# Moving the tiles of a two-block attention kernel so that TensorE's operands start on 256-byte boundaries of SBUF

## The chip, the cores and the metric

One core of a Trainium2 chip runs the program. The metric is the device time of one execution in microseconds. The kernel before took 1605.19 us (median of 3 runs, 1604.76 to 1605.27).

## The reference

Two transformer blocks follow each other on a 512 x 2048 float32 input. The first is sliding-window attention with sinks: a norm, one projection to queries, keys, values and a gate, 32 heads of 64 with a window of 128, a gated output and an output projection, added to the input. The second puts 16 learned tokens ahead of the 512 and runs differential attention (8 heads) and latent attention with rotary positions (8 heads) side by side, again gated, projected and added, with a last norm.

```
h = rms_norm(x, swa_norm);  q, k, v, gate = split(h @ w_in)
o = softmax_with_sink(q k^T / 8 + bias, window 128) v
x = x + (o * silu(gate)) @ w_out
h = concat(meta, x);  proj = rms_norm(h) @ w_in_2          # 528 rows, 5952 columns
oA = rms_norm((softmax(q1 k1) - lam * softmax(q2 k2)) vA) ;  oB = softmax(qB kB + rope) vB
h = h + concat(oA * silu(gA), oB * silu(gB)) @ w_out_2
y = rms_norm(h, final_norm)
```

## The kernel before, in words

Every large product is made of three matmuls. An operand is kept as two float32r tiles, a rounded high part and the low rest (names ending in h and l, or `xh1`/`xl1`, `xh2`/`xl2`), and a product is high x high + high x low + low x high, through the helper `mm` (L111). Weights come in by DMA on SP's queue as 512 KB pieces `raw`; ScalarE copies a 128 x 512 unit to `wh` (L158) and VectorE makes `wl` (L168). In each matmul one operand stands in the array (a 128 x 128 block, which TensorE loads with a LDWEIGHTS instruction) and the other moves through it (up to 512 columns).

The stages run one after another on TensorE; attention pieces are woven into the projections by a queue of deferred functions (`Flow`), and VectorE, ScalarE and TensorE work in the order of the program text.

1. Keys, values and queries of block one (to about 300 us): the weights move, the input `xh1`/`xl1` stands (`proj_n`, L288 on). 960 matmuls with 512 columns, and woven in the window attention: scores with 256 columns (`kth`, `ktl` move, `qt` stands), transposes, and 112 products p x v with 512 columns.
2. Gate of block one, `gate1` (about 300 to 509 us): the input moves, the weights stand (`proj_t`). 768 matmuls with 512 columns.
3. Output of block one, `out1` (509 to 694 us): weights move, `ogh1`/`ogl1` stand. 768 with 512 columns. Its result is transposed into `xh2`/`xl2`, the input of block two.
4. Latent projections (`c_cq`, `c_ck`, `c_pe`): weights move and `xh2`/`xl2` stand (192 with 512 columns, 240 with 320), then 48 with 512 columns.
5. Heads of block two (about 800 to 1270 us): `diff_qk` (384 with 512 columns and 768 with 264), `diff_v` (768 with 264), `mla_proj` (96 with 512 columns, others with 256 and 264), with the attention of 16 heads woven in.
6. Gates of block two, `gate2` (about 1270 to 1420 us): `xh2`/`xl2` move, weights stand. 768 with 512 columns. Rows k = 0 to 15 of the input are taken in turn, 12 matmuls for one k (k = 0, 1 and 14, 15 in another order).
7. Output of block two, `out2` (from 1420 us): weights move, `ogh2`/`ogl2` stand. 720 with 512 columns and 96 with 256. Its first 7 units of weights still come from the tiles that all earlier stages use; then `open_ring` gives it a ring of 16 new `wh` and 16 new `wl`.

Of the 8615 matmuls that the page counts, 4864 have 512 columns; the others are shorter or are transposes.

The positions of tiles in SBUF come out of the code in this way. A pool with side "left" grows up from the low end of SBUF, one with side "right" down from the high end; tiles of a pool lie one behind the other in the order in which the code first asks for them, each rounded up to 32 bytes. So sizes in the code give the positions. The remainder of the byte address by 256 in the program before, called the phase here:

| tile | phase |
|---|---|
| `raw`, `wh`, `wl` (all stages) | 160 |
| `wh`, `wl` of the ring in `out2` | 192 |
| `xh1`, `xl1` | 160 |
| `ogh1`, `ogl1` | 224 |
| `ogh2`, `ogl2` | 192 |
| `xh2`, `xl2` | 160; one row k takes 528 floats = 2112 bytes = 8 x 256 + 64, so the 512 token columns of row k start at phase 224 + 64k: 224, 32, 96, 160, 224, ... |
| `kth`, `ktl`, the values `v` | 64 |
| `qt` | 192 |
| `pth`, `ptl` of block one | 224 |
| `cqh`, `cql`, `ckh` | 160 |
| `identr` | 128 |

A block of 128 columns of a standing operand is 512 bytes and a weight unit 2048 bytes, so all blocks of a tile have its phase (rows of `xh2` apart). The halves of 264 columns in `diff_qk` and `diff_v` start at the row and 1056 bytes behind it.

Of the kernel before, what the change touches and what calls it, by code (L numbers as in the profile page):

```python
# [9 lines left out]
F32 = mybir.dt.float32  # L10
F32R = mybir.dt.float32r
# [7 lines left out]
KT = 16  # L19
S = 512  # L20
NTB = 4
META = 16
LK = S + META
HALF = LK // 2
EPS = 1e-6
BIG = 1e30
ZROW = 384
# [8 lines left out]
def mixer_kernel(ctx, tc, x, rel_bias, w_in1, q_gain, k_gain, sinks, w_out1,  # L36
# [37 lines left out]
    P = Pools()  # L74
    dram = P("dram", space=DRAM)
    const = P("const", side="left")
    wp = P("w", side="left")
    ps_pj = P("ps_pj", bufs=4, space=PSUM)
    ps_sc = P("ps_sc", bufs=2, space=PSUM)
    ps_tp = P("ps_tp", bufs=2, space=PSUM)  # L80
# [183 lines left out]
    F = Flow()  # L264
# [97 lines left out]
    rstd2 = const.tile([128, NTB], F32, name="rstd2")  # L362
    mrstd = const.tile([128, 1], F32, name="mrstd")
    nlam = const.tile([128, 1], F32, name="nlam")
    G1, G2, GQ, GKV, GSUB = 0, 16, 32, 36, 38

    xa = P("xa", side="left")
# [150 lines left out]
    p1 = P("p1", side="right")  # L518
# [2 lines left out]
    vt = [p1.tile([128, 4, 2, 64], F32R, name=f"v{t}") for t in range(NTB)]  # L521

    def hstat():
        return p1.tile([128, 8], F32, tag="st", name="st", bufs=4)

    def qn_t():
        return p1.tile([128, 512], F32, tag="qn", name="qn", bufs=4)
# [110 lines left out]
    def swa_pieces():  # L638
        items = [(g, t, i) for g in range(4) for t in range(NTB) for i in range(2)]
        st = {}  # L640

        def s1(n, j):
            g, t, i = items[n]
            if t == 1 and i == 0 and j == 0 and g < 3:
                swa_bias(g + 1)
            if j == 0:
                st[n] = dict(
                    p=p1.tile([128, 4, 256], F32, tag="p", name="p", bufs=2),
                    nm=p1.tile([128, 4], F32, tag="nm", name="nm", bufs=3),
                    sm=p1.tile([128, 4], F32, tag="sm", name="sm", bufs=3))  # L650
            p, nm, sm = st[n]["p"], st[n]["nm"], st[n]["sm"]
            qt = qts[g, t]
            bias = biases[g, i]
            h0 = 8 * g + 4 * i
            k0 = max(t - 1, 0) * 128
            lo = 128 if t == 0 else 0
            w = 256 - lo
            sc = ps_sc.tile([128, 2, 256], F32, tag="sc", name="sc")
            for a in range(2):
                h = 4 * i + 2 * j + a  # L660
                mm(sc[:, a, :], qt[:, h, :], kth[:, g, k0:k0 + 256], True, False)
                mm(sc[:, a, :], qt[:, h, :], ktl[:, g, k0:k0 + 256], False, True)
            for a in range(2):
                b = 2 * j + a
                nc.vector.tensor_tensor_reduce(  # L665
                    out=p[:, b, :w], in0=sc[:, a, :w], in1=back(bias, b, w), scale=1.0,
                    scalar=nsink[:, h0 + b:h0 + b + 1], op0=ALU.add, op1=ALU.min,
                    accum_out=nm[:, b:b + 1])
                nc.scalar.activation(out=p[:, b, :w], in_=p[:, b, :w], func=ACTF.Exp, scale=-1.0,  # L669
                                     bias=nm[:, b:b + 1], accum_out=sm[:, b:b + 1])  # L670
            if j == 1:
                es = p1.tile([128, 4], F32, tag="es", name="es", bufs=3)
                st[n]["es"] = es
                nc.vector.tensor_tensor(out=es, in0=nm, in1=nsink[:, h0:h0 + 4], op=ALU.subtract)
                nc.scalar.activation(out=es, in_=es, func=ACTF.Exp)
# [125 lines left out]


    xb = P("xb", side="left")
    xh2 = xb.tile([128, KT, LK], F32R, tag="h", name="xh2")
    xl2 = xb.tile([128, KT, LK], F32R, tag="l", name="xl2")
    XR = {}

    def open_xr():
# [12 lines left out]
    def meta_in():  # L821
        xr_p = XR["p"]
        mt = xr_p.tile([16, D], F32, name="mt")
        nc.sync.dma_start(out=mt, in_=meta)
        mps = xr_p.tile([128, KT, 16], F32, name="mps")
        nc.sync.dma_start(out=mps, in_=meta_t)
        mss = xr_p.tile([16, 1], F32, name="mss")
        mjunk = xr_p.tile([16, D], F32, name="mjunk")

        def rest():  # L830
            nc.scalar.activation(out=mjunk, in_=mt, func=ACTF.Square, accum_out=mss)
            rsqrt_mean(mrstd[:16], mss, D, rows=16)
            mg = xr_p.tile([128, KT, 16], F32, name="mg")
            nc.vector.tensor_tensor(
                out=mg, in0=mps, in1=gcols[:, G2:G2 + 16].unsqueeze(2).to_broadcast([128, KT, 16]),
                op=ALU.mult)
            split(xh2[:, :, 0:16], xl2[:, :, 0:16], mg)
            row_bcast(rb2[:, 0:16], mrstd, 16)
        F.defer(20, rest)

    def out1(c):
        if c:
            XR[c] = load_r(c)
        ps = [pj() for _ in range(NTB)]

        def evac(t):
            xr_p, ss2, xr = XR["p"], XR["ss"], XR[c]
            nc.vector.tensor_tensor(out=xr[:, t, :], in0=ps[t], in1=xr[:, t, :], op=ALU.add)
            squares(xr, c, ss2, xr_p, t)
            if t == NTB - 1:  # L850
                for i in range(4):
                    F.defer(4 + 2 * i, lambda i=i: x_to_t(xr, c, i, xh2, xl2, META, G2))
                if c == 3:
                    F.defer(13, finish)
                F.defer(14, lambda: nc.sync.dma_start(
                    out=x1_d[:, c * 512:(c + 1) * 512].rearrange("(t p) c -> p t c", p=128), in_=xr))

        def finish():
            ssr2 = XR["p"].tile([128, NTB], F32, name="ssr2")
            nc.vector.tensor_reduce(out=ssr2, in_=XR["ss"], axis=AX.X, op=ALU.add)  # L860
            rsqrt_mean(rstd2, ssr2, D)
            F.defer(6, lambda: [row_bcast(rb2[:, 16 + t * 128:16 + (t + 1) * 128], rstd2[:, t:t + 1])
                                for t in range(NTB)])

        proj_n(c_o1[c], KT, lambda k, b: (og["h"][:, k, b * 128:(b + 1) * 128],
                                          og["l"][:, k, b * 128:(b + 1) * 128]), ps, evac)
# [9 lines left out]


    def tok(k, b):
        c = slice(META + b * 128, META + (b + 1) * 128)
        return xh2[:, k, c], xl2[:, k, c]  # L880

    def tok_m(k, b):
        if b < NTB:
            return tok(k, b)
        return xh2[:, k, 0:128], xl2[:, k, 0:128]

    B2 = {}

    def open_b2():
        P.close("xr", "og1")  # L890
        ms = P("ms", side="left")
        B2["cqh"] = ms.tile([128, 4, S], F32R, name="cqh")
        B2["cql"] = ms.tile([128, 4, S], F32R, name="cql")
        CW = 2 * LK + 256
        B2["ckh"] = ms.tile([128, CW], F32R, name="ckh")
        B2["ckl"] = ms.tile([128, CW], F32R, name="ckl")
        for n_ in ("ckh", "ckl"):
            nc.gpsimd.memset(f32(B2[n_][:, 2 * LK:]), 0.0)
        B2["kph"] = ms.tile([128, LK], F32R, name="kph")
        B2["kpl"] = ms.tile([128, LK], F32R, name="kpl")  # L900
        B2["qpt"] = ms.tile([128, 8, S], F32R, name="qpt")
        p2c = P("p2c", side="right")
        lat = P("lat", side="right")
        for nm_, shape, src in (
                ("relm", [128, LK], c_rel), ("mask", [128, LK], c_mask),
                ("cosq", [128, NTB, 32], c_cos[META:, :].rearrange("(t p) c -> p t c", p=128)),
                ("sinq", [128, NTB, 32], c_sin[META:, :].rearrange("(t p) c -> p t c", p=128)),
                ("cosm", [16, 32], c_cos[:META, :]), ("sinm", [16, 32], c_sin[:META, :])):
            t = (p2c if shape[1] == LK else lat).tile(shape, F32, name=nm_)
            nc.sync.dma_start(out=t, in_=src)  # L910
            B2[nm_] = t
        B2["rsub"] = p2c.tile([128, 32], F32, name="rsub")
        B2["p2c"] = p2c
        B2["lat"] = lat
# [160 lines left out]
        return [lambda k: src(k, slice(0, HALF)), lambda k: src(k, slice(HALF, LK))]  # L1075

    def xk(k, c):
        return xh2[:, k, c], xl2[:, k, c]

    def ckx(k, c):  # L1080
# [5 lines left out]
    def mla_proj(h):  # L1086
        p2 = B2["p2"]
# [3 lines left out]
        ql = p2.tile([128, S], F32R, tag="mql", name="mql", bufs=1)  # L1091
        kh = p2.tile([128, LK], F32R, tag="mkh", name="mkh", bufs=1)
        kl = p2.tile([128, LK], F32R, tag="mkl", name="mkl", bufs=1)
        cq_, ckv = c_m[h]
        pq = pj()
        proj_t(cq_, 4, [(slice(0, 128), [(pq, lambda k: (B2["cqh"][:, k, :], B2["cql"][:, k, :]))],
# [40 lines left out]
    def diff_qk(h):  # L1137
# [5 lines left out]
        def qev():  # L1143
# [3 lines left out]
            qd = [p2.tile([128, S], F32R, tag=f"dq{i}", name=f"dq{i}", bufs=1) for i in range(2)]  # L1147
            ql = B2["qlz"]
            ks = [p2.tile([128, LK], F32R, tag=f"dk{i}", name=f"dk{i}", bufs=1) for i in range(2)]
            heads["d", h] = (qd, ql, ks, None)  # L1150
            t = wide()
            nc.vector.scalar_tensor_tensor(out=t[:, :S], in0=pq, scalar=-0.125 * 2.0 ** (h + 1),
# [253 lines left out]
    def gate2(c):  # L1406
# [17 lines left out]
        def evac(m):  # L1424
            if c == 0 and m == 0:
# [3 lines left out]
                ogp = P("og2", side="right")  # L1429
                G["h"] = ogp.tile([128, KT, S], F32R, name="ogh2")  # L1430
                G["l"] = ogp.tile([128, KT, S], F32R, name="ogl2")
                G["sw"] = ogp.tile([128, 1], F32, name="sw")
                nc.vector.tensor_scalar(out=G["sw"], in0=gcols[:, GSUB:GSUB + 1],
                                        scalar1=(1.0 - LAM0) * 0.5, scalar2=None, op0=ALU.mult)
                G["gp"] = P("gp2", side="right")
# [90 lines left out]
        out2(c)  # L1526
    F.flush_later()
    phase(None)
    P.close("fin", "wr", "og2", "ps_tp", "ps_sc", "ps_pj", "w", "const", "dram")

# [54 lines left out]
```

## Time and profile before

| | |
|---|---|
| median of 3 runs | 1605.19 us |
| the profiled execution's own time | 1604.56 us |
| its span, from the first to the last instruction | 1602.8 us |
| TensorE matmuls, busy | 1585.7 us, 99% of the span |
| VectorE, ScalarE, GpSimd, busy | 917.8, 727.9, 110.1 us |
| mean of what the DMA moved | 108 GB/s |
[...]

The profiled execution ends 0.63 us below the median, and 1.8 us of it lie outside the span. A matmul's length in the profile (0.39 us with 512 columns) is longer than the step from its start to the next start, because matmuls overlap in the array: the step is what counts, and the timeline gives it as the difference of two start times over the number of matmuls between them.

### The profile page before, as it was taken

What the parts mean: (1) busy time and instruction counts of PE and PEld (TensorE: products, weight loads), DVE (VectorE), ACT (ScalarE), POOL (GpSimd) and SP (SyncE); (2) the same over time, 40 slices, a digit from 0 to 9 for tenths busy, and PEclk for the clock granted to TensorE, in tenths of its full rate; (3) what the DMA queues carried; (4) which work ended last, traced back from release to release, by engine and by line L of the source; (5) the groups of instructions that cost most, each with busy time, mean ns of one, the idle gap of its engine ahead of it and who ended that gap; (6) DMA issues with size and microseconds to landing.
All of it is one profiled execution on the core that took longest, in us unless ns stands there. A gap on an engine that the chain in (4) does not pass through costs nothing.

```text
span 1602.8 us, 23242 instructions
## 1 busy us (share of the span) xinstructions
PE 1585.7 (99%) x8615; PEld 1358.8 (85%) x8615; DVE 917.8 (57%) x2218; ACT 727.9 (45%) x1608; POOL 110.1 (7%) x165
## 2 busy tenths in 40 slices
PE   9999999999999999999999999999999999999998
PEld 7788888887888788888899999999999888888887
DVE  6658888887454333333666766656657455455332
ACT  5556766775333323333455454545545333334322
POOL 3330320300000000000100000000000000000001
PEclk9999999999999999999999999999999999999999
DMA  6422323325333534342332322232232364365312
GB/s 231 146 79 83 104 81 96 84 69 171 120 104 104 161 123 142 110 134 67 80 96 67 92 71 79 74 86 76 57 106 66 109 203 127 95 221 173 105 40 106
DMA packets 144674, 173.78 MB, mean 108 GB/s; under 512 B 13088, under 2 KB 82080, under 8 KB 144032
## 3 DMA queue, kind: packets, MB, share of 16 engines
q1 hardware_dynamic: 144560, 172.29, 35.1%
q8 instruction: 68, 1.11, 0.3%
q14 instruction: 46, 0.38, 0.1%
HBM read 155.41 MB, written 16.84 MB: 107 GB/s over the span
## 4 chain that ended last, share of the span: by engine, by line
PE 91%; DVE 4%; ACT 2%; DMA 1%; issue 1%; POOL 0%; SPq 0%; ACTq 0%; POOLq 0%; DVEq 0%
PE pj L111 78%; PE sc L111 4%; PE pv L111 4%; PE tp L694 1%; PE tp L1290 1%; DMA xt<-in_x_t_dram 1%; DVE wl L168 1%; PE tp L622 1%; PE tp L425 0%; DVE xl L274 0%; PE sqs L1344 0%; PE ck_m L111 0%; ACT p L669 0%; DVE dql L272 0%; ACT wh L158 0%
## 5 line engine op out<-in xcount | busy, mean ns | idle before, releaser
L168 DVE TENSOR_TENSOR wl<-raw,wh 128x512 fp32r<-128x512 f32 (+1 forms) x488 | 336.0, 695 | 404.9 <-ACT wh L158 403.0
L158 ACT ACTIVATE wh<-raw 128x512 fp32r<-128x512 f32 (+1 forms) x488 | 298.6, 619 | 401.4 <-PE pj L111 351.4
L111 PE MATMUL pj<-xh,wh 128*128 128x512 f32 (+1 forms) x1152 | 363.6, 352 | 0.0
L111 PE MATMUL pj<-xh,wl 128*128 128x512 f32 (+1 forms) x1152 | 356.5, 345 | 0.6 <-DVE wl L168 0.6
L111 PE MATMUL pj<-xl,wh 128*128 128x512 f32 (+1 forms) x1152 | 356.3, 345 | 0.0
L111 PEld LDWEIGHTS pj<-xh,wh 128*128 128x128 f32 x1152 | 205.5, 188 | 27.8 <-ACT wh L158 0.4
L111 PEld LDWEIGHTS pj<-xh,wl 128*128 128x128 f32 x1152 | 199.7, 188 | 27.6 <-DVE wl L168 1.0
L111 PEld LDWEIGHTS pj<-xl,wh 128*128 128x128 f32 x1152 | 199.9, 188 | 19.5
L111 PE MATMUL pj<-wh,ogh 128*128 128x512 f32 (+1 forms) x528 | 204.6, 388 | 0.0
L111 PE MATMUL pj<-wl,ogh 128*128 128x512 f32 (+1 forms) x528 | 203.7, 386 | 0.0
L111 PE MATMUL pj<-wh,ogl 128*128 128x512 f32 (+1 forms) x528 | 203.6, 386 | 0.0
L111 PE MATMUL pj<-wh,xh 128*128 128x512 f32 (+1 forms) x448 | 175.3, 391 | 0.9 <-DVE v L274 0.7
L111 PE MATMUL pj<-wh,xl 128*128 128x512 f32 (+1 forms) x448 | 171.1, 382 | 1.2 <-DVE xl L274 1.1
L111 PE MATMUL pj<-wl,xh 128*128 128x512 f32 (+1 forms) x448 | 170.5, 380 | 0.1
L1253 ACT ACTIVATE p2t<-p2t,nm 128x144 f32<-128x144 f32 (+3 forms) x96 | 55.2, 575 | 140.0 <-DVE nm L1249 139.9
L111 PEld LDWEIGHTS pj<-wh,ogl 128*128 128x128 f32 x528 | 99.2, 188 | 21.3
L111 PEld LDWEIGHTS pj<-wh,ogh 128*128 128x128 f32 x528 | 99.2, 188 | 20.8
L111 PEld LDWEIGHTS pj<-wl,ogh 128*128 128x128 f32 x528 | 99.2, 188 | 20.7
L111 PEld LDWEIGHTS pj<-wh,xl 128*128 128x128 f32 x448 | 84.1, 188 | 18.8 <-DVE xl L274 2.9
L111 PEld LDWEIGHTS pj<-wh,xh 128*128 128x128 f32 x448 | 84.2, 188 | 13.9 <-DVE v L274 1.1
L111 PEld LDWEIGHTS pj<-wl,xh 128*128 128x128 f32 x448 | 84.3, 188 | 12.1 <-DVE wl L168 0.5
L669 ACT ACTIVATE p<-p,nm 128x256 f32<-128x256 f32 (+1 forms) x128 | 60.7, 475 | 60.6 <-DVE nm L665 60.5
(308 smaller groups left out, 2075.9 us busy)
## 6 DMA issues: line engine op xcount, KB each, us to landing
raw<-in_swa_w_in_dram SPq DMA_DIRECT2D x72, 512.0 KB, 3.7
raw<-in_w_in_dram SPq DMA_DIRECT2D x56, 512.0 KB, 3.8
raw<-in_swa_w_out_dram SPq DMA_DIRECT2D x32, 512.0 KB, 3.7
raw<-in_w_in_dram SPq DMA_DIRECT2D x128, 128.0 KB, 2.6
raw<-in_w_out_dram SPq DMA_DIRECT2D x32, 512.0 KB, 3.6
oin<-ot_d SPq DMA_DIRECT2D x8, 1024.0 KB, 7.1
bias<-bm_d SPq DMA_DIRECT2D x8, 512.0 KB, 4.9
ot_d<-ot SPq DMA_DIRECT2D x32, 128.0 KB, 1.8
```

Of the source, the lines that this page charges most:

```text
L111: nc.tensor.matmul(o, lhsT=l, rhs=r, start=start, stop=stop)
L158: nc.scalar.activation(out=h[:, :n], in_=self.raw_t[r][:, o:o + n], func=ACTF.Copy)
L168: nc.vector.tensor_tensor(out=l[:, :n], in0=self.raw_t[r][:, o:o + n], in1=f32(h[:, :n]), op=ALU.subtract)
L622: nc.tensor.transpose(tp[:, h, :].bitcast(F32R), qs[:, 4 * i + h].rearrange("p a b -> p (a b)"), identr)
L669: nc.scalar.activation(out=p[:, b, :w], in_=p[:, b, :w], func=ACTF.Exp, scale=-1.0, bias=nm[:, b:b + 1], accum_out=sm[:, b:b + 1])
L694: nc.tensor.transpose(tp[:, b, :], st[n]["p"][:, b, kb * 128:(kb + 1) * 128], ident)
L1253: nc.scalar.activation(out=p[:, :w], in_=p[:, :w], func=ACTF.Exp, scale=-1.0, bias=m, accum_out=sums[:, comp:comp + 1])
L1290: nc.tensor.transpose(tp[:, kb, :], p[:, kb * 128:(kb + 1) * 128], ident)
```

## The change

No instruction is added or removed. Unused tiles are put between others, `sw` (one column) moves into the `const` pool under the name `subw`, the statistics tile `st` doubles its size, and a row of `xh2`/`xl2` takes 576 floats (2304 bytes, 9 x 256), with the 16 learned tokens at column 48 and the 512 tokens at column 64.

```diff
+LKP, MO = 576, 48
@@
+    top = P("top", side="right")
+    top.tile([128, 56], F32, name="top_pad")
@@
+    subw = const.tile([128, 1], F32, name="subw")
+    const.tile([128, 16], F32, name="const_pad")
@@
     def hstat():
-        return p1.tile([128, 8], F32, tag="st", name="st", bufs=4)
+        return p1.tile([128, 16], F32, tag="st", name="st", bufs=4)[:, :8]
@@ swa_pieces, s1
                 es = p1.tile([128, 4], F32, tag="es", name="es", bufs=3)
+                if n == 0:
+                    p1.tile([128, 56], F32, name="p1_pad")
@@
-    xh2 = xb.tile([128, KT, LK], F32R, tag="h", name="xh2")
-    xl2 = xb.tile([128, KT, LK], F32R, tag="l", name="xl2")
+    xh2 = xb.tile([128, KT, LKP], F32R, tag="h", name="xh2")
+    xl2 = xb.tile([128, KT, LKP], F32R, tag="l", name="xl2")
@@ meta_in
-            split(xh2[:, :, 0:16], xl2[:, :, 0:16], mg)
+            split(xh2[:, :, MO:MO + META], xl2[:, :, MO:MO + META], mg)
@@ out1
-                    F.defer(4 + 2 * i, lambda i=i: x_to_t(xr, c, i, xh2, xl2, META, G2))
+                    F.defer(4 + 2 * i, lambda i=i: x_to_t(xr, c, i, xh2, xl2, MO + META, G2))
@@ tok, tok_m, xk
-        c = slice(META + b * 128, META + (b + 1) * 128)
+        c = slice(MO + META + b * 128, MO + META + (b + 1) * 128)
-        return xh2[:, k, 0:128], xl2[:, k, 0:128]
+        return xh2[:, k, MO:MO + 128], xl2[:, k, MO:MO + 128]
     def xk(k, c):
+        c = slice(MO + c.start, MO + c.stop)
@@ open_b2
+        ms.tile([128, 32], F32, name="ms_pad")
         B2["qpt"] = ms.tile([128, 8, S], F32R, name="qpt")
@@ mla_proj
+        if h == 0:
+            p2.tile([128, 32], F32, name="mk_pad")
@@ diff_qk
+            if h == 0:
+                p2.tile([128, 32], F32, name="dk_pad")
@@ gate2
-                G["sw"] = ogp.tile([128, 1], F32, name="sw")
+                G["sw"] = subw
```

## Rows read from the trace of the kernel before

**Rows 1.** The page: span, busy time and instructions of each engine, chain by line.
```profile
span 1602.8 us, 23242 instructions
...
PE 1585.7 (99%) x8615; PEld 1358.8 (85%) x8615; DVE 917.8 (57%) x2218; ACT 727.9 (45%) x1608; POOL 110.1 (7%) x165
...
PE pj L111 78%; PE sc L111 4%; PE pv L111 4%; PE tp L694 1%; PE tp L1290 1%; DMA xt<-in_x_t_dram 1%; DVE wl L168 1%; PE tp L622 1%; PE tp L425 0%; DVE xl L274 0%; PE sqs L1344 0%; PE ck_m L111 0%; ACT p L669 0%; DVE dql L272 0%; ACT wh L158 0%
```

**Rows 2.** The waits of TensorE, the longest of nine: us in total, times, longest.
```profile
PE tp L1290 <- DVE p2t L1269: 1.9, 4, 0.6
```

**Rows 3.** Busy us (x instructions) of PE, PEld, DVE, ACT, POOL; clock, DMA.
```profile
1300.00:1400.00 100.00, 100.00 (x434) 81.14 (x433) 49.30 (x76) 31.12 (x53) 0.00 (x0) 1.00 0.39 117
1460.00:1560.00 100.00, 100.00 (x443) 82.84 (x442) 39.58 (x60) 30.09 (x60) 0.00 (x0) 1.00 0.26 88
```

**Rows 4.** Timeline of TensorE in `gate1` (start us, length us), 45 steps apart.
```profile
429.66 0.39 PE L111 MATMUL pj<-xh,wl 128*128 128x512 f32 x1
...
439.86 0.39 PE L111 MATMUL pj<-xh,wl 128*128 128x512 f32 x1
```

**Rows 5.** Timeline of TensorE in `out1`, 44 steps apart.
```profile
539.72 0.40 PE L111 MATMUL pj<-wl,ogh 128*128 128x512 f32 x1
...
549.99 0.40 PE L111 MATMUL pj<-wh,ogh 128*128 128x512 f32 x1
```

**Rows 6.** Timeline in `out2`: old weight tiles (24 steps), then the ring (27 steps).
```profile
1433.62 0.40 PE L111 MATMUL pj<-wl,ogh 128*128 128x512 f32 x1
...
1439.22 0.40 PE L111 MATMUL pj<-wl,ogh 128*128 128x512 f32 x1
...
1559.83 0.39 PE L111 MATMUL pj<-wh,ogl 128*128 128x512 f32 x1
...
1565.95 0.39 PE L111 MATMUL pj<-wh,ogl 128*128 128x512 f32 x1
```

**Rows 7.** Timeline in `gate2`: first matmul of rows k = 5 to 10, 12 steps each.
```profile
1344.41 0.40 PE L111 MATMUL pj<-xh,wh 128*128 128x512 f32 x1
...
1347.21 0.39 PE L111 MATMUL pj<-xh,wh 128*128 128x512 f32 x1
...
1350.00 0.39 PE L111 MATMUL pj<-xh,wh 128*128 128x512 f32 x1
...
1352.74 0.40 PE L111 MATMUL pj<-xh,wh 128*128 128x512 f32 x1
...
1355.51 0.40 PE L111 MATMUL pj<-xh,wh 128*128 128x512 f32 x1
...
1358.30 0.39 PE L111 MATMUL pj<-xh,wh 128*128 128x512 f32 x1
```

**Rows 8.** Timeline at the end of `out2`, 256 columns, 93 steps apart.
```profile
1583.17 0.28 PE L111 MATMUL pj<-wh,ogh 128*128 128x256 f32 x1
...
1594.33 0.28 PE L111 MATMUL pj<-wh,ogh 128*128 128x256 f32 x1
```

**Rows 9.** Timeline in `diff_v`: 6 matmuls of 264 columns and what follows, twice.
```profile
912.05 0.40 PE L111 MATMUL pj<-xh,wh 128*128 128x264 f32 x2
...
912.77 0.34 PE L111 MATMUL sc<-dk,dq 128*128 128x400 f32 x1
...
913.14 0.41 PE L111 MATMUL pj<-xh,wh 128*128 128x264 f32 x2
...
913.87 0.40 PE L111 MATMUL pj<-xh,wh 128*128 128x512 f32 x1
```

**Rows 10.** Timeline of block one's scores: 4 matmuls of 256 columns, then a projection.
```profile
299.03 0.28 PE L111 MATMUL sc<-kth,qt 128*128 128x256 f32 x1
...
299.50 0.40 PE L111 MATMUL pj<-wh,xh 128*128 128x512 f32 x1
```

**Rows 11.** Timeline of the weight loads (PEld) in `out2`.
```profile
1559.83 0.19 PEld L111 LDWEIGHTS pj<-wh,ogh 128*128 128x128 f32 x1
```

More of the change, by code (lines that the diff above doesn't have):

```diff
@@ L1528, in mixer_kernel @@
     phase(None)
-    P.close("fin", "wr", "og2", "ps_tp", "ps_sc", "ps_pj", "w", "const", "dram")
+    P.close("fin", "wr", "og2", "ps_tp", "ps_sc", "ps_pj", "top", "w", "const", "dram")
 def _constants():
```

## The prediction

> **What bounds the kernel now.** The page first: matmuls cover 1585.7 of 1602.8 us, no other engine is above 57%, and the chain that ended last runs over the projections' matmuls (L111, `pj`) for 78% of the span [rows 1]. The view of waits says whether TensorE ever stands still for somebody: its longest entry is 1.9 us in total, and all nine come to 8.1 us [rows 2]. So the time is a sum of matmul steps, and a change that touches no instruction can gain only if a step gets shorter. Third, the windows: 100 us of `out2` hold 443 matmuls, 100 us of `gate2` hold 434, at the same granted clock 1.00, both with nothing but 512 columns, no engine near its limit and the DMA at 0.26 and 0.39 [rows 3]. The same instruction has two prices. The timeline tells them apart:
>
> - `gate1`: 10.20 us over 45 steps, 226.7 ns [rows 4].
> - `out1`: 10.27 us over 44, 233.4 ns [rows 5].
> - `out2`, from the old weight tiles: 5.60 us over 24, 233.3 ns; from the ring, the same standing operands: 6.12 us over 27, 226.7 ns [rows 6].
> - `gate2`, row by row of its input: k = 5, 6, 8, 9 take 2.80, 2.79, 2.77, 2.79 us for 12, that is 233.3, 232.5, 230.8, 232.5 ns; k = 7 takes 2.74 us, 228.3 ns [rows 7].
>
> Beside the table of phases one rule fits all of them: the step is short where the moving and the standing operand have the same phase. `gate1` has 160 against 160, the ring 192 against 192, row k = 7 of `gate2` 160 against 160. `out1` has 160 against 224, the head of `out2` 160 against 192, rows 5, 6, 8, 9 have 32, 96, 224, 32 against 160. The head of `out2` is the best witness: only the phase of the weights differs from what follows it in the same loop. The weight load for the next matmul starts within 0.01 us of the matmul ahead of it [rows 6, 11], so both operands are being read from SBUF at once; that their relative place sets a price is my reading, the price itself is in the rows.
>
> [...] The rows show 233.3 and 226.7 ns in one loop [rows 6]. [...]
>
> **The change, part by part.** By the sizes, `subw` and its pad end the `const` pool so that `raw`, `wh`, `wl`, `xh1`, `xl1`, `xh2` all start at phase 0; the 56 floats on top put `ogh1`, `ogh2`, the ring and the pools of the right side there; 2304 bytes per row give every row's token columns phase 0. Against the step of equal phases:
>
> 1. `out1`: 768 matmuls, all unequal now. 768 x (233.4 - 226.7) = 5.1 us [rows 4, 5].
> 2. The input of block two: `gate2` 768, `diff_qk` 384, the latent query 192, together 1344 with 512 columns. Three rows in four are unequal: 1008 x (232.3 - 226.7), with 232.3 as the mean of the four rows, = 5.6 us. The equal quarter has 228.3, as its neighbours spill into it: 336 x 1.6 = 0.5 us [rows 4, 7].
> 3. Head of `out2`: 7 units x 12 = 84, x 6.6 = 0.6 us [rows 6].
> 4. Block one's p x v, 112 (224 against 64), and some 170 last matmuls ahead of transposes or scores, whose next standing block has another phase: 282 x 4 to 6.6 ns = 1.1 to 1.9 us; I take 1.2, as the start differences around them are too coarse to say more.
> 5. Matmuls of 256 and 264 columns, some 2400. Those of 264 step at 720/6 = 120.0 ns with phases 160 and 192 against 160, and at 730/6 = 121.7 with 224 and 0 [rows 9]; 256 columns with equal phases step at 120.0 [rows 8]. These look tied to something of about 120 ns whatever the phase. Afterwards the halves lie at 192 and 224 against 0. I take 0; if all went to 120.0 the gain would be 1776 x 1 = 1.8 us, if all went up by 1.7 the loss 3.0.
> 6. Block one's scores, 256 matmuls: 470/4 = 117.5 ns now with 64 against 192 [rows 10]; with equal phases perhaps the 120.0 of rows 8: +0.6 us.
> 7. The empty tiles cost no instruction. The wider rows of `xh2` push the left side 6.2 KB up, onto addresses whose last users finished long before (block one's buffers, when the latent stage opens its pools), so I expect no new wait; all of TensorE's waits now are 8.1 us [rows 2], and one more like the longest would cost 0.6. VectorE and ScalarE do the same work; at 49% and 31% in `gate2` [rows 3] they keep ahead of matmuls that are 2% faster.
>
> Sum: -5.1 - 5.6 - 0.5 - 0.6 - 1.2 + 0 + 0.6 = -12.4 us. The profiled execution is 1604.56 us, 0.63 under the median, so 1592.2 there and 1592.8 against the median. Since spill between stages will not vanish everywhere (the equal quarter at 228.3 instead of 226.7), I give 0.9 us back: 1593.7.
>
> **Rivals.**
>
> - The start itself counts, not the difference, and whole 256-byte starts are better than anything seen. In `out2`, 512 columns step at 226.7 and 256 at 120.0 [rows 6, 8]: 106.7 ns for 256 columns, so a step is its columns plus 13.3 ns even with equal phases. If that rest went too for all 4864, the time would be 1593.7 - 64.7 = 1529; half of it, 1561. For: no pair at 0 against 0 stands in the trace. Against: 160 and 192 give the same 226.7, though only 192 is a multiple of 64. [...] Chance 0.08.
> - Nothing changes, 1605: the short steps belong to the loops, not to the places, or the layout does not come out as the sizes say. For: `gate1` and `out1` also differ in which operand moves. Against: rows 6 and 7 show both prices within one loop. Chance 0.07.
> - Slower: the place counts, and phase 0 is a bad one, for instance because every stream of TensorE then begins at the same spot as every tile that VectorE and ScalarE write. Price: the roughly 2700 matmuls that are equal now go from 226.7 to 233.4, +18 us, to 1623, with the unequal ones left where they are. It decides from a step of about 229.3 ns at 0 against 0, the mean of today's two classes (2720 at 226.7, 2144 at 232.5). Against: in `gate1` `raw`, `wh`, `wl` and `xh1` already share one phase, at 226.7 [rows 4]. Chance 0.05.
>
> **How the numbers follow.** The forecast has 0.80; its own range is 1587 to 1601: upward 7.8 us if all steps settle at the 228.3 of row 7 rather than 226.7 (4864 x 1.6), downward the bounds of parts 4 and 5 and the parts that I gave back or set at a loss (0.7 + 1.8 + 0.9 + 0.6 = 4.0) and as much again for stages whose steps I did not look at. That is the range I give: the rivals outside it hold 0.20. A measurement of this kernel can tell 0.2% from no change, 3.2 us: faster 0.88 (the forecast and the first rival), same 0.07, slower 0.05.
>
> **What would show it.** Right: `out1` and the head of `out2` step at 226.7 to 227 ns; in `gate2` row 7 no longer stands out and 100 us hold 440 or more matmuls; `gate1` and the ring keep 226.7, the 264 columns 120 to 122; waits of TensorE stay near 8 us. Wrong: `out1` still at 233 (no effect), `gate1` or the ring at another step than 226.7 (the place itself counts), or new waits of TensorE at the opening of a pool.

## The result, and the profile after

The changed kernel takes 1593.85 us (median of 6 runs, 1593.21 to 1595.24), the kernel before 1604.97 us beside it (median of 6, 1603.92 to 1605.63). The ratio is 0.9932, with a 95% interval of 0.9921 to 0.9943: 11.1 us less. The profiled execution took 1594.24 us, with a span of 1592.5 us. That is 10.3 us less than the span of before.

The page of the changed kernel, beside [rows 1]: span, busy time of the engines, chain by line. Line 111 of before is line 114 here.

```profile
span 1592.5 us, 23242 instructions
...
PE 1573.6 (99%) x8615; PEld 1357.9 (85%) x8615; DVE 918.3 (58%) x2218; ACT 728.4 (46%) x1608; POOL 110.4 (7%) x165
...
PE pj L114 76%; PE sc L114 4%; PE pv L114 4%; PE tp L701 1%; DVE wl L171 1%; PE tp L1303 1%; DMA xt<-in_x_t_dram 1%; PE tp L627 1%; ACT wh L161 0%; DMA oin<-ot_d 0%; DMA raw<-in_swa_w_in_dram 0%; PE tp L430 0%; DVE xl L277 0%; PE sqs L1357 0%; PE ck_m L114 0%
```

The counts are the same, and so is the order of TensorE's instructions. VectorE and ScalarE are as busy as before; TensorE alone has lost 12.1 us. So most of the difference must lie in matmul steps, and the windows over stretches that hold only 512 columns show it (columns as in [rows 3]):

```profile
1290.00:1390.00 100.00, 100.00 (x443) 82.81 (x442) 50.04 (x77) 31.73 (x53) 0.00 (x0) 1.00 0.41 125
1450.00:1550.00 100.00, 100.00 (x443) 82.81 (x442) 39.54 (x60) 29.84 (x59) 0.00 (x0) 1.00 0.26 86
```

`gate2` now fits 443 matmuls into 100 us where it had 434; the ring of `out2` had 443 and still has. The granted clock is 1.00 in both, as before.

The timeline of TensorE, at the same instructions as [rows 4 to 6] and at the first matmul of rows k = 5, 7, 8 and 10 of `gate2` [rows 7]:

```profile
429.81 0.39 PE L114 MATMUL pj<-xh,wl 128*128 128x512 f32 x1
...
440.01 0.39 PE L114 MATMUL pj<-xh,wl 128*128 128x512 f32 x1
...
539.17 0.39 PE L114 MATMUL pj<-wl,ogh 128*128 128x512 f32 x1
...
549.14 0.39 PE L114 MATMUL pj<-wh,ogh 128*128 128x512 f32 x1
...
1336.31 0.39 PE L114 MATMUL pj<-xh,wh 128*128 128x512 f32 x1
...
1341.75 0.39 PE L114 MATMUL pj<-xh,wh 128*128 128x512 f32 x1
...
1344.47 0.39 PE L114 MATMUL pj<-xh,wh 128*128 128x512 f32 x1
...
1349.91 0.39 PE L114 MATMUL pj<-xh,wh 128*128 128x512 f32 x1
...
1423.58 0.39 PE L114 MATMUL pj<-wl,ogh 128*128 128x512 f32 x1
...
1429.02 0.39 PE L114 MATMUL pj<-wl,ogh 128*128 128x512 f32 x1
...
1572.95 0.28 PE L114 MATMUL pj<-wh,ogh 128*128 128x256 f32 x1
...
1584.10 0.28 PE L114 MATMUL pj<-wh,ogh 128*128 128x256 f32 x1
```

`gate1`: 10.20 us over 45 steps, 226.7 ns, unchanged. `out1`: 9.97 over 44, 226.6 ns, where it was 233.4. `gate2`: 5.44 us for the 24 steps from k = 5 to 7, 2.72 for the 12 of k = 7, 5.44 for the 24 from k = 8 to 10, 226.7 ns everywhere; row 7 no longer stands out. Head of `out2`: 5.44 over 24, 226.7 ns, where it was 233.3. The 256 columns at the end: 11.15 over 93, 119.9 ns, as before.

Because TensorE's instructions have the same order, the two traces can also be laid over each other: the start of an instruction after, less its start before, is what was gained (minus) or lost (plus) up to there. From the rows here and [rows 4 to 8]: +0.15 us at the first of `gate1`, -0.55 and -0.85 at the two of `out1`, -8.10 at k = 5 and -8.39 at k = 10 of `gate2`, -10.04 and -10.20 in the head of `out2`, -10.23 in its last 256 columns. By stage, worked out in the same way from the first and last matmul of each:

| stretch | gain (us) |
|---|---|
| block one's projections and scores | 1.03 |
| `gate1` | -1.17 |
| `out1` | 4.44 |
| latent projections | 0.71 |
| heads of block two | 1.72 |
| `gate2` | 2.93 |
| `out2` | 0.56 |

The loss in `gate1` is one wait. The waits of TensorE, longest in total first (us in total, times, longest; the view has ten entries, 10.5 us in sum, where before had nine with 8.1):

```profile
PE pj L405 <- DVE identr L400: 2.9, 1, 2.9
PE tp L1303 <- DVE p2t L1282: 2.0, 4, 0.7
PE pj L114 <- ACT wh L161: 1.1, 1, 1.1
```

The third stands in no entry of before, and none of the eight runs below has it above 0.4 us, so it belongs to this execution rather than to the layout. The first, at the very start, was 1.6 us before. It is 2.7 to 2.9 us in all seven runs below that are edits of the changed kernel and 1.6 in the eighth, so it comes with the change. The start of the two traces shows how, before and then after:

```profile
1.35 0.23 DVE L395 CAST identr<-eye 128x128 fp32r<-128x128 f32 x1 [0.47 <-POOL eye masks.py:199]
1.63 1.97 PE L400 MATMUL pj<-identr 128*128 128x128 f32 x8 [1.63 <-DVE identr L395]
...
2.58 0.15 DVE L1446 TENSOR_SCALAR subw<-gcols 128x1 f32<-128x1 f32 x1 [1.70 <-DMA gcols<-in_gains_dram]
2.65 0.22 DVE L400 CAST identr<-eye 128x128 fp32r<-128x128 f32 x1
2.93 0.69 PE L405 MATMUL pj<-identr 128*128 128x128 f32 x2 [2.93 <-DVE identr L400]
```

The instruction that fills `sw` ran at 1282.8 us before, early in `gate2`. Filling `subw`, in the pool that is open from the start, it is the third instruction of VectorE, although the text has it at line 1446: here VectorE doesn't follow the order of the text. It waits for the DMA of `gcols`, the copy of `identr` stands behind it, and TensorE's first matmul starts 1.3 us later. Whether these 1.3 us are lost in the end isn't shown. The steps that waits for `xh` and `xl` lengthen got shorter by more than that: the matmul that started at 34.45 us before comes 1.35 us earlier after the change. So the 1.03 us of block one in the table are mostly shorter waits, not shorter steps.

### The profile page after: what moved, and what is told of

Read it like the earlier page. It is cut to its first block, busy times and chain, and to the rows that moved or that the text cites. A ratio compares the mean times of both kernels' runs of the same rounds, so it can differ in the third digit from the quotient of the medians.

```text
span 1592.5 us, 23242 instructions
## 1 busy us (share of the span) xinstructions
PE 1573.6 (99%) x8615; PEld 1357.9 (85%) x8615; DVE 918.3 (58%) x2218; ACT 728.4 (46%) x1608; POOL 110.4 (7%) x165
## 4 chain that ended last, share of the span: by engine, by line
PE 90%; DVE 4%; ACT 3%; DMA 2%; issue 1%; POOL 0%; SPq 0%; ACTq 0%; POOLq 0%; DVEq 0%
PE pj L114 76%; PE sc L114 4%; PE pv L114 4%; PE tp L701 1%; DVE wl L171 1%; PE tp L1303 1%; DMA xt<-in_x_t_dram 1%; PE tp L627 1%; ACT wh L161 0%; DMA oin<-ot_d 0%; DMA raw<-in_swa_w_in_dram 0%; PE tp L430 0%; DVE xl L277 0%; PE sqs L1357 0%; PE ck_m L114 0%
```

## The experiments

Eight kernels ran. Three of them ran five times and have an interval; the others are one execution, read by their steps. All are edits of the changed kernel, except the last. Where a mean is given for a stage without rows, it is over its 512-column steps with at least twelve of that width ahead, taken from their start times, without the lengthened steps (260 ns and more) beside waits and transposes.

**All tiles moved to another place, distances kept.** Every tile behind the two pads has its phase moved on by 96: all operands of the long products go to phase 96, none to a multiple of 256 (`identr`, ahead of the pads, stays at 128).

```diff
-    top.tile([128, 56], F32, name="top_pad")
+    top.tile([128, 96], F32, name="top_pad")
-    const.tile([128, 16], F32, name="const_pad")
+    const.tile([128, 40], F32, name="const_pad")
```

> Every tile of the changed kernel moved by 96 bytes, so that moving and standing operands still have one phase, 96 instead of 0. Theory (the difference of the two phases sets the step): long runs of 512 columns step at 226.7 ns as in the changed kernel, time 1592.5 to 1595.5 us. Rival (each operand's own start counts, multiples of 256 are good ones): the steps go back to 231 to 234 ns, time 1603 to 1615 us. Rival (the gain came from VectorE, ScalarE or the DMA on aligned tiles): time about 1600 to 1605 us.

Measured: 1593.24 us (1592.60 to 1594.22), ratio to before 0.9928 (0.9915 to 0.9942), so the same as the change. The timeline in `out1`, 44 steps:

```profile
538.17 0.39 PE L114 MATMUL pj<-wl,ogh 128*128 128x512 f32 x1
...
548.15 0.39 PE L114 MATMUL pj<-wh,ogh 128*128 128x512 f32 x1
```

9.98 us, 226.8 ns a step at 96 against 96, where 0 against 0 had 226.6. Where the tiles start together doesn't count.

**Only the weights moved, by 128 bytes.** All starts stay multiples of 128, but the weights (`raw`, `wh`, `wl`, the ring) are at phase 128 and the activations at 0.

```diff
-    const.tile([128, 16], F32, name="const_pad")
+    const.tile([128, 48], F32, name="const_pad")
+    xa.tile([128, 32], F32, name="xa_pad")
+    xb.tile([128, 32], F32, name="xb_pad")
+                if self.pool is not wp and not self.padded:
+                    self.pool.tile([128, 32], F32, name="wr_pad")
```

> Only the weight tiles (raw, wh, wl, ring) moved to phase 128; all other operands stay at 0. Every start is still a multiple of 128. Theory: all projections of 512 columns step at about 232 to 233 ns, also gate1 and the ring of out2, which had 226.7 both before and after; 4700 x about 5 ns on top of the changed kernel gives 1613 to 1623 us, slower than the kernel before. Rival (own starts, multiples of 128 good enough): about 1594 us.

Measured: 1615.26 us, span 1613.5. The timeline in `gate1` (45 steps), then in the ring (27 steps), both of which had the short step before and after the change:

```profile
433.43 0.39 PE L114 MATMUL pj<-xh,wl 128*128 128x512 f32 x1
...
443.92 0.40 PE L114 MATMUL pj<-xh,wl 128*128 128x512 f32 x1
...
1569.97 0.39 PE L114 MATMUL pj<-wh,ogl 128*128 128x512 f32 x1
...
1576.26 0.40 PE L114 MATMUL pj<-wh,ogl 128*128 128x512 f32 x1
```

10.49 over 45 is 233.1 ns, 6.29 over 27 is 233.0. This kernel does everything that the change does except one distance, and is 10.4 us slower than the kernel before (1604.87 in these runs). A round address by itself is worth nothing (233 ns at 128 against 0); how far apart the operands start counts. It also speaks for 256 as the period: in the changed kernel the rows of `xh2`, 2304 bytes (9 x 256) apart, are all at the short step of 226.7 ns, while tiles 128 apart, at 233, aren't.

**Distances from 0 to 240 in steps of 16.** The rows of `xh1`/`xl1` get 2064 bytes, so row k lies at phase 16k.

```diff
-    xh1 = xa.tile([128, KT, S], F32R, tag="h", name="xh1")
+    xh1 = xa.tile([128, KT, S + 4], F32R, tag="h", name="xh1")[:, :, :S]
```

> Rows of xh1 and xl1 take 2064 bytes, so row k starts at phase 16k; weights stay at 0. Theory: within gate1 row 0 steps at 226.7 ns and the others at 229 to 234, each row with its own price by its difference, and out1, gate2, out2 stay at 226.7; 15 of 16 rows of 1728 matmuls get about 5 ns more, so time 1598 to 1603 us. Rival (own starts, multiples of 64 good): rows 4, 8, 12 as fast as row 0. Rival (only the standing or only the moving operand counts): the price shows in gate1, where xh1 moves, but not in the first stage, where it stands, or the other way round.

Measured: 1598.27 us, span 1596.5. In `gate1`, over the same 45 steps:

```profile
431.63 0.40 PE L114 MATMUL pj<-xh,wl 128*128 128x512 f32 x1
...
442.06 0.40 PE L114 MATMUL pj<-xh,wl 128*128 128x512 f32 x1
```

10.43 us, 231.8 ns. By row the means lie between 230 (distance 64) and 235 (208). Row 4, at 64, is the fastest, but rows 8 and 12, at 128 and 192, have 233, and none comes near 226.7. Even row 0, whose distance is zero, has 231.5 and not the 226.7 that was expected. It alternates with row 1; the block that it uses and the block loaded beside it are both at distance zero. The first stage, where `xh1` stands instead of moving, rises too (232.3 for `wh` on `xh1`, where the change has 227.2), while `out1` and `out2`, which don't touch `xh1`, keep 226 to 227.

**A pitch of 2080 bytes for the weight units.** Within `wh` and `wl`, unit after unit moves on by 32 bytes.

```diff
-                h = self.pool.tile([128, 512], F32R, tag="wh", name="wh", bufs=self.wb)
+                h = self.pool.tile([128, 520], F32R, tag="wh", name="wh", bufs=self.wb)
```

(and the same for `wl`)

> The weight tiles lie 2080 bytes apart: the four wh at phases 0, 32, 64, 96, the four wl at 128, 160, 192, 224, the ring through all eight. Everything else stays at 0. Theory: the step of a matmul follows the difference between what it moves and the block that is loaded while it moves, which is the next matmul's: in gate1, with wh at 0, xh with wh (next wh) steps at 226.7, xl with wh (next wl, at 128) is slower, and xh with wl (next wh, at 0) is fast again. Rival (its own standing block counts): xl with wh is fast and xh with wl is slow. Time for both 1610 to 1622 us.

Measured: 1612.23 us, span 1610.5. All distances step at 229 to 236 ns. The pairs with equal phases (the unit of `wh` at 0) among unequal neighbours step at 231.8 and 232.8 in `gate1`, at 234.2 and 230.1 in `out1`: an equal pair alone isn't enough. The 231.8 are those of `xh,wh`, where the block loaded next is the same one, so equal too. Neither reading of the expectation came: with `wh` at 0 neither `xh,wh` nor `xl,wh` is at 226.7.

**Only `wl` moved by 128 bytes.** Two pads of 128 bytes in each pool, one between the `wh` and the `wl` and one behind the `wl`; `wh` and the activations stay at phase 0.

```diff
+        def pad(self, which):
+            key = (which, self.pool is wp)
+            if key not in self.padded:
+                self.padded.add(key)
+                self.pool.tile([128, 32], F32, name="pad_" + which)
```

> Only the wl tiles move to phase 128, wh and all others stay at 0. In gate1 the order is xh with wh, xl with wh, xh with wl. Theory as first put (moving operand against the block loaded beside it, the next one): xl with wh is slow, the other two step at 226.7 ns. Rival (own standing block): xh with wl is slow alone. Third reading, from the run with weights 2080 bytes apart, where pairs of equal phase among unequal neighbours stepped at 230 to 231: a step is short only where all neighbours share the phase, so none of the three settles at 226.7. In out1 (wh, wl, wh move, og stands at 0) all readings give at least the wl step as slow. Time: first and second reading 1600 to 1604 us, third 1604 to 1614 us.

Measured: 1608.10 us, span 1606.2. Here the three matmuls of a product have three different situations, so the timeline in `gate1` is shown step by step:

```profile
430.91 0.39 PE L114 MATMUL pj<-xh,wh 128*128 128x512 f32 x1
431.14 0.40 PE L114 MATMUL pj<-xl,wh 128*128 128x512 f32 x1
431.37 0.40 PE L114 MATMUL pj<-xh,wl 128*128 128x512 f32 x1
431.61 0.39 PE L114 MATMUL pj<-xh,wh 128*128 128x512 f32 x1
431.83 0.40 PE L114 MATMUL pj<-xl,wh 128*128 128x512 f32 x1
432.07 0.40 PE L114 MATMUL pj<-xh,wl 128*128 128x512 f32 x1
432.30 0.39 PE L114 MATMUL pj<-xh,wh 128*128 128x512 f32 x1
432.53 0.40 PE L114 MATMUL pj<-xl,wh 128*128 128x512 f32 x1
432.76 0.40 PE L114 MATMUL pj<-xh,wl 128*128 128x512 f32 x1
432.99 0.39 PE L114 MATMUL pj<-xh,wh 128*128 128x512 f32 x1
```

From `xh,wh` to the next start: 0.23 + 0.22 + 0.23 = 0.68 us for three, 227 ns. From `xl,wh`: 0.70, 233; from `xh,wl`: 0.70, 233. Over the stage the means are 226.8, 232.4 and 234.2, and in `gate2` 226.6, 232.5 and 234.2. So the matmul whose own block is equal but whose next block isn't (`xl,wh`, with `wl` being loaded) is slow, and so is the one whose own block is unequal although the next is equal (`xh,wl`); the one with both equal is short here even between slow neighbours. In the gates, then, neither the block being loaded nor the block in use is the whole answer, and the third reading fails as well, although the time lies in its range. Where the weights move it is less tidy: in the ring `wl` steps at 234.1 and the two `wh` keep 226.7 and 225.9, but in `out1`, with the same order of the three, `wl` has 234.3 and the two `wh` 233.2 and 228.8, though both have equal phases with their own block and the next. Row 0 of the run with 2064 bytes was such a case too, at 231.5. So a distance of zero to both blocks is not enough beside unequal ones, and what decides there stays open.

**Four constant distances, one for each activation.** `ogh2`/`ogl2` 8 bytes, `xh1`/`xl1` 16, `xh2`/`xl2` 32, `ogh1`/`ogl1` 64, each by a view that starts a few floats into a larger tile.

```diff
-                G["h"] = ogp.tile([128, KT, S], F32R, name="ogh2")
+                G["h"] = ogp.tile([128, KT * S + 64], F32R, name="ogh2")[:, 2:2 + KT * S].rearrange("p (k c) -> p k c", k=KT)
```

> Weights at 0; xh1/xl1 start 16 bytes behind a multiple of 256, ogh1/ogl1 64, xh2/xl2 32, ogh2/ogl2 8, each the same for all rows. Theory (any difference of the phases costs, by place): long runs step above 226.7 ns in all of gate1, out1, gate2 and out2, 229 to 234. Rival (the price begins at some step of 32 or 64 bytes): out2 at 8 bytes and gate1 at 16 stay at 226.7, out1 at 64 does not. Time by the theory 1608 to 1620 us, by the rival 1596 to 1604 us.

Measured: 1611.80 us, span 1610.0. The ring of `out2`, at 8 bytes, 27 steps:

```profile
1567.17 0.39 PE L114 MATMUL pj<-wh,ogl 128*128 128x512 f32 x1
...
1573.40 0.39 PE L114 MATMUL pj<-wh,ogl 128*128 128x512 f32 x1
```

6.23 us, 230.7 ns. The stage means are 230.5 to 230.7 at 8 bytes, 231.5 to 231.8 at 16 (`gate1`), 233.1 to 233.6 at 32 (`gate2`), 233.3 to 233.5 at 64 (`out1`). None of these distances is small enough: two floats cost about 4 ns, 32 bytes about as much as 64, or as the 128 of the moved weights (233.0 and 233.1). Each distance was tried in a stage of its own, so small differences between them may be the stage's.

**The row pitch of `xh2` back to 2112 bytes, all else kept.**

```diff
-LKP, MO = 576, 48
+LKP, MO = LK, 0
```

> Only the row pitch of xh2/xl2 is undone (528 floats, learned tokens at column 0), all pads stay. Theory: gate2, diff_qk and the latent query fall back to their unequal steps in three rows of four, everything else stays: 1593.85 + 4.3 (what these stages gained) = 1597 to 1599 us. Rival (the pitch does nothing of its own, the pads do it all): 1593 to 1595 us.

Measured: 1599.10 us (1598.26 to 1600.57), ratio to before 0.9967 (0.9954 to 0.9979): 0.1 us above what was expected, and about half of the gain given back. The window over `gate2`, as after:

```profile
1290.00:1390.00 100.00, 100.00 (x434) 81.14 (x433) 50.61 (x79) 31.73 (x55) 0.00 (x0) 1.00 0.42 127
```

434 matmuls again, the number of before. Against the profiled execution of the change, `gate2` lost 2.9 us, the latent projections 0.7 and the heads 1.9; of this the matmuls of 264 columns took 1.2. So the row pitch is what they gained by.

**The kernel before with two edits.** The pitch of 576 floats, and one pad of 64 bytes at the high end; no other pad. The weights, `xh1`, `xh2` and `ogh1` are now at 160, `ogh2` and the ring at 128: none of these starts at a multiple of 256. `sw` stays where it was.

```diff
+LKP, MO = 576, 48
@@
+    P("top", side="right").tile([128, 16], F32, name="top_pad")
@@
-    xh2 = xb.tile([128, KT, LK], F32R, tag="h", name="xh2")
-    xl2 = xb.tile([128, KT, LK], F32R, tag="l", name="xl2")
+    xh2 = xb.tile([128, KT, LKP], F32R, tag="h", name="xh2")
+    xl2 = xb.tile([128, KT, LKP], F32R, tag="l", name="xl2")
```

> The kernel before with the row pitch and one pad of 64 bytes at the high end alone: weights and xh1 and xh2 at 160, ogh1 at 160, ogh2 and the ring at 128; no tile of these at a multiple of 256. Theory: all long runs have equal phases, only the head of out2 (84 matmuls, 160 against 128) does not, time 1593.5 to 1596 us. Rival (multiples of 256 are needed): 1600 to 1605 us.

Measured: 1595.56 us (1594.61 to 1598.42), ratio to before 0.9949 (0.9935 to 0.9962). All long runs step at 226 to 227.5 ns but one, the head of `out2` (160 against 128), over 24 steps:

```profile
1423.70 0.40 PE L113 MATMUL pj<-wl,ogh 128*128 128x512 f32 x1
...
1429.30 0.40 PE L113 MATMUL pj<-wl,ogh 128*128 128x512 f32 x1
```

5.60 us, 233.3 ns, exactly as before [rows 6]. Two edits bring 9.1 of the 11.1 us; the intervals of the two ratios overlap, so the times don't settle what the rest of the padding is worth. No run was clearly faster than the changed kernel.

## Why the prediction was right, and where its terms were off

The forecast was 1593.7 us and the median is 1593.85. The steps foreseen for the long runs came: 226.6 in `out1`, 226.7 in the head of `out2`, an even 226.7 over the rows of `gate2` with 443 matmuls in 100 us, `gate1` and the ring unchanged. All three rivals are out: the place itself doesn't count, for better or worse (the run at phase 96 has the change's time), and the layout does what the sizes say. One sum of the range doesn't come out (4.0 us and as much again below 1593.7 is 1585.7, not 1587), but nothing hung on it. That the two times agree to 0.15 us is partly luck, because terms were missed on both sides:

- Part 1, `out1`, 5.1 us: 4.4 measured. The 233.4 ns of [rows 5] came from a long run; over all 768 the mean step fell by 5.8 ns (181.2 to 176.8 us in all), since those beside transposes gained less.
- Part 2, the input of block two, 6.1 us: 4.3. `gate2` gave 3.0 (its share of the sum was 3.5), the latent query 0.65 (of 0.9), and `diff_qk` 0.6 (of 1.7). This is the step that failed most, and it shows what was wrong with "short where moving and standing operand have the same phase": an equal pair is not enough. In `diff_qk` the 512-column matmuls come in threes between matmuls of 264. The timeline of the changed kernel there, the last of the 264 columns, then the first and last of a run of six with 512 (three of `diff_qk` and three p x v woven in), then what follows them:

```profile
960.71 0.40 PE L114 MATMUL pj<-xh,wl 128*128 128x264 f32 x2
960.95 0.39 PE L114 MATMUL pj<-xh,wh 128*128 128x512 f32 x1
...
962.10 0.40 PE L114 MATMUL pv<-pth,mvl 128*128 128x512 f32 x1
962.33 0.34 PE L114 MATMUL pv<-pth,mvh 128*128 128x384 f32 x1
```

  1.38 us for six, 230 ns, with equal phases throughout. Over the whole trace the median of a 512-column step right behind 264 columns is 232 (94 steps), behind 256 columns 233 (71), behind 400 columns 235 (10); from the twelfth of a run on, more than nine in ten lie at 226 or 227. The prediction priced every matmul with equal phases by [rows 4], a run of hundreds. There is a rival: the 264 columns ahead start at 192 and 224 against 0, so unequal phases just ahead could do the same. But 62 of the steps behind 256 columns have, by the sizes, equal phases on both sides, and their median is 233 too. That a shorter matmul ahead is the cause is read from these groups; no run changed only that.
- Part 3, the head of `out2`, 0.6: 0.56.
- Part 4, p x v and the last matmuls of a run, 1.2: 0.4, probably for the same reason as `diff_qk`; they stand beside shorter ones.
- Part 5, the 264 columns, 0 with bounds of -1.8 and +3.0: -1.4. [rows 9] did show 120.0 and 121.7, and they were taken for one value. Of the steps between two others of 264 columns, 1386, the mean fell from 121.9 to 120.9 ns, and with the old pitch it was 121.8. So the place counts here too, but not by the rule: after the change 1207 of these 1386 lie at distances 192 and 224, not at zero, and step at 120.7 and 121.0, while those at zero had 121.3 before. A part of the gain is that few are left at distances 96 to 160, which had 122.2 to 123.2 before; the rest stays open.
- Part 6, block one's scores, +0.6: +0.1. The timeline of the changed kernel at the four of [rows 10] still has 0.47 us, 117.5 ns:

```profile
298.00 0.28 PE L114 MATMUL sc<-kth,qt 128*128 128x256 f32 x1
...
298.47 0.40 PE L114 MATMUL pj<-wh,xh 128*128 128x512 f32 x1
```

- Part 7, no new wait, put at nothing: this step failed. The wait at the very start grew from 1.6 to 2.9 us through the moved `subw`; the prediction had looked at the empty tiles and the wider rows, not at the instruction that fills `subw`. The other new wait, 1.1 us in `gate1`, is of one execution.
- The 0.9 us given back for spill between stages was the right kind of caution and too small: parts 1, 2 and 4 together stayed 3.3 us short, the 264 columns and part 6 brought 1.9 back, and block one's start 0.8, where less waiting for `xh` and `xl` stood against the later first matmul; the one wait in `gate1` took 1.2 of the profiled execution.

The prediction's reason, that the weight load reads SBUF beside the moving operand, remains argued: the runs show that the relation of the two addresses, with that of the matmuls around them, sets the price (226.6 to 226.8 ns in the long runs where all start at one phase, 230.7 to 233.4 where they start apart), and not what in the chip makes it so.

## What to carry to other kernels

When TensorE is the bound and one matmul shape shows two step times at the same clock (here 226.7 and 233.4 ns at 1.00), put the addresses of the moving and the standing operand beside the steps; a pad of a few dozen bytes (64 here) or a row pitch that is a multiple of 256 (2304 here) may be all it takes (here two edits, 0.5%). Match the two operands to each other modulo 256 (226.8 ns at 96 against 96), not to a round address (233.1 at 128 against 0), and do so for all matmuls of a run, since an equal pair beside unequal ones can be slow (231.8 in `gate1` of the run with weight units 2080 bytes apart). Price the gain by runs of the length that the stage really has, since behind a shorter matmul much of it isn't there (medians of 232 to 235 ns in place of 226.7). And look at the instructions that a moved tile takes along: one of them can come ahead of the first matmul (here that one's wait grew from 1.6 to 2.9 us).

## What the hardware showed that was not expected

- The step answers to very small distances: 226.7 ns at 0, 230.6 at 8 bytes, 231.7 at 16, 233 at 32 and 64, 233 in `gate1` and the ring at 128.
- In the gates the own block and the next one both count: with `wl` alone 128 bytes away, 226.8, 232.4 and 234.2 ns in turn. But zero distance to both isn't enough everywhere: 233.2 and 228.8 in `out1` of the same run.
- Right behind a matmul of 256 or 264 columns the median of a 512-column step is 233 and 232 ns, and 226 to 227 is reached only in a longer run.
- For the matmuls of 264 columns a distance of zero is nothing special: 121.3 ns before the change, where 192 and 224 had 121.4 and 121.6 and 128 was the slowest at 123.2.
- Even in long runs it is 226.7 ns for 512 columns and 119.9 for 256, which is 106.8 for the 256 more, so by these two some 13 ns (226.7 - 2 x 106.8) beyond the columns remain. What they are wasn't tried.
